# Two chained layers on one core: the second layer's input projection by seven products for half of k

## The chip, the cores and the metric

The kernel runs on 1 core of one Trainium2 chip. The metric is the device time of one execution in microseconds (us): 2892.36 us median of 3 runs (2892.21 to 2892.92). Less is better.

## The reference, cut to what matters

Two layers run one after the other on a sequence of 512 tokens with model width 2048. The first is a gated delta rule layer with cross attention. The second, which the change touches, is this (cut):

```python
u = rmsnorm(h, norm_w[l])                                   # (1, 512, 2048)
proj = jnp.einsum('bsd,dc->bsc', u, w_in[l])                # (1, 512, 8200)
(ml_q, ml_k, ml_v, ml_o, ml_z, ml_i, ml_f,
 hg_q, hg_f, hg_i, hg_g) = jnp.split(proj, split_points, axis=-1)
...
h_a = mlstm_chunkwise(q_a, k_a, v_a, i_pre, f_pre)          # 4 heads
y_a = jax.nn.sigmoid(ml_o) * rmsnorm(h_a) * jax.nn.silu(ml_z)
...
h_b = hgrn2_chunkwise(q_b, k_b, logf_b, i_b)                # 8 heads
y_b = rmsnorm(h_b) * jax.nn.silu(hg_g)
y = jnp.concatenate([y_a, y_b], axis=-1)
h = h + jnp.einsum('bsc,cd->bsd', y, w_out[l])
e = jnp.einsum('bsr,rd->bsd', p[l], w_pe[l])
gate = jax.nn.sigmoid(jnp.einsum('bsd,de->bse', rmsnorm(h), w_pg[l]))
out = rmsnorm(h + gate * e)
```

All in float32.

## The kernel before, in words

Everything is kept transposed: 128 features on the partitions, the 512 tokens (`T`) along the free axis. A projection is a list of jobs. One job (class `Job`) is one output tile of 128 features by 512 tokens, accumulated in one PSUM bank over `kt` tiles of k (16 for the second layer's input projection). To keep float32 accuracy at the speed of the `float32r` type, both operands are split in a high and a low part, hi = float32r(x) and lo = x - hi, and each k takes three matmuls: hi·xh, hi·xl, lo·xh (`_unit`). So a tile of the second input projection is 48 matmuls of 128x512.

Weights come in pieces of `KC` = 4 k-tiles (128x512 elements, 256 KB). `_pump` issues the load of a piece into one of `RAW` = 6 buffers named raw (on the SyncE queue, SP), makes hi by a copy on ScalarE (ACT) and lo by a subtraction on VectorE (DVE), into `SPL` = 5 buffers each.

The order of the work is written out by a planner that runs while the program is built (class `Driver`). It holds a clock for each engine, with a cost for each kind of operation, and issues whichever task of highest priority is ready by these clocks, and otherwise the next matmul unit. So every engine's order of instructions is fixed, and is right to the extent that the costs are. The costs know of no influence of one engine on another. A task is a Python generator; where it says `yield`, the planner may put other work ahead of its next part.

Working tiles (128x512) come from a pool of `NSLOT` = 75 slots, PSUM has 8 banks. The 16 normalised input tiles of the second projection (`X2`), each as hi and lo, hold 32 slots.

The second projection has 65 jobs: the gates i and f (`w_if`, half as wide), 16 tiles for the four mLSTM heads (`ml_task`), 24 for the eight HGRN2 heads (`hg_task`: f, q, i for each head), then 8 `w_mlo`, 8 `w_mlz` and 8 `w_hgg` gate tiles. `scaled` reads a finished bank on DVE and multiplies with the row norm. An `hg_task` goes through seven levels: on each, DVE and ACT make a tile z and TensorE (PE) makes a product named pg from it. Head results stay in slots until the gate tiles have multiplied them (`evac_gate`), and `split_task` makes the operands of the output projection (`Y2`, tiles ph and pl).

GpSimd (POOL) has next to nothing to do in this stage. It sums squares at the start of the kernel (tile xsum).

Of the kernel before, what the change touches and what calls it, by code (L numbers as in the profile page):

```python
# [9 lines left out]
F32 = mybir.dt.float32  # L10
# [13 lines left out]
RAW, SPL = 6, 5  # L24
NSLOT = 75
LV, LP = 0.3, 0.3
AHEAD = 1.5
# [37 lines left out]
class Job:  # L65

    def __init__(self, w, x, evac, n=T, prio=5.0, begin=None, c0=0):
        self.w, self.x, self.evac, self.n, self.prio, self.begin = w, x, evac, n, prio, begin
        self.cols = slice(c0, c0 + n)
        self.kt = w.shape[1]  # L70
        self.narrow = w.shape[2] < 128
        self.ps = None
        self.drop = False

# [8 lines left out]
class Driver:  # L83
# [5 lines left out]
    def __init__(self, tc, wp, psp, sp):  # L89
        self.tc, self.nc, self.wp, self.psp, self.sp = tc, tc.nc, wp, psp, sp  # L90
        self.clk = dict(pe=0.0, act=0.0, dve=0.0, pool=0.0, sp=1.2)
        self.dq = 0.0
        self.tau = 0.0
        self.tasks = []
        self.units = []
        self.pieces = []
        self.i_unit = self.i_dma = self.i_hi = self.i_spl = self.i_mm = 0
        self.spl_end = []
# [6 lines left out]
        self.nslot = 0  # L105
        self.table = None
        self.reader, self._bank = {}, []
        self.small_mm = False
        self.nhead, self.head = 0, None
# [192 lines left out]
    def add(self, *jobs):  # L302

        pcs = {j: [] for j in jobs}
        for c0 in range(0, max(j.kt for j in jobs), KC):
            for j in jobs:
                if c0 >= j.kt:
                    continue
                n = min(KC, j.kt - c0)
                p = len(self.pieces)  # L310
                self.pieces.append((j, c0, n))
                for k in range(c0, c0 + n):
                    self.units.append((j, k, p, k == c0 + n - 1, j is jobs[-1]))

    def _pump(self):
        while self.i_dma < len(self.pieces):
            r = self.i_dma - RAW
            if r >= 0 and (r >= self.i_spl or self.spl_end[r][1] > self.clk["pe"]):
                break
            j, c0, n = self.pieces[self.i_dma]  # L320
            raw = self.wp.tile([128, KC, 128], F32, tag="raw", bufs=RAW, name="raw")
            self.nc.sync.dma_start(out=raw[:, :n, :j.w.shape[2]], in_=j.w[:, c0:c0 + n])
            self.pieces[self.i_dma] = (j, c0, n, raw, self.land(n * 128 * j.w.shape[2]))
            self.i_dma += 1
            if self.i_dma <= self.nhead:
                self.head(self.i_dma)
        while self.i_hi < self.i_dma and self.i_hi < self.i_mm + SPL:
            j, c0, n, raw, tau = self.pieces[self.i_hi]
            if tau > self.clk["pe"] and self.i_hi > self.i_mm:
                break  # L330
            hi = self.wp.tile([128, KC, 128], F32R, tag="hi", bufs=SPL, name="hi")
            self.tau = tau
            m = j.w.shape[2]
            self.act(hi[:, :n, :m], raw[:, :n, :m], AF.Copy)
            self.pieces[self.i_hi] = (j, c0, n, raw, hi, self.tau)
            self.i_hi += 1
        while self.i_spl < self.i_hi:
            j, c0, n, raw, hi, tau = self.pieces[self.i_spl]
            if tau > max(self.clk["pe"], self.clk["dve"]) and self.i_spl > self.i_mm:
                break  # L340
            self.tau = tau
            if j.narrow:
                lo = None
                self.tt(hi[:, :n, 64:], raw[:, :n, :64], hi[:, :n, :64], SUB)
            else:
                lo = self.wp.tile([128, KC, 128], F32R, tag="lo", bufs=SPL, name="lo")
                self.tt(lo[:, :n], raw[:, :n], hi[:, :n], SUB)
            self.pieces[self.i_spl] = (j, c0, n, hi, lo, self.tau)
            self.spl_end.append((self.i_spl, self.tau))
            self.i_spl += 1  # L350

    def _unit_tau(self):

        j, k, p, _, _ = self.units[self.i_unit]
        if p >= self.i_spl or not j.x.f[k].done:
            return None
        t = max(self.pieces[p][5], j.x.f[k].tau)
# [4 lines left out]
        return t  # L362

    def _unit(self):
        j, k, p, last_of_piece, last_job = self.units[self.i_unit]
        self.i_unit += 1
        _, c0, _, hi, lo, _ = self.pieces[p]
# [7 lines left out]
        c = j.cols  # L375
        self.tau = 0.0
        self.mm(j.ps, hi[:, k - c0], xh[:, c], start=(k == 0), stop=False)
        self.tau = 0.0
        self.mm(j.ps, hi[:, k - c0], xl[:, c], start=False, stop=j.narrow and k == j.kt - 1)
        if not j.narrow:  # L380
            self.tau = 0.0
            self.mm(j.ps, lo[:, k - c0], xh[:, c], start=False, stop=(k == j.kt - 1))
        self.tau = self.clk["pe"]
        if last_of_piece:
            self.i_mm += 1
            self.pieces[p] = None
        if j.drop and last_job and (k + 1) % j.x.per == 0:
            self.free(xh, xl)
        if k == j.kt - 1:
            self.tau = self.clk["pe"] + 0.2  # L390
            self.spawn(j.evac(j), j.prio)
# [5 lines left out]
    def run(self):  # L397
        while True:
# [20 lines left out]
            if self.i_unit < len(self.units):  # L419
                ut = self._unit_tau()  # L420
                if ut is not None:
                    if ut <= now:
                        self._unit()
                        continue
                    nxt = ut if nxt is None else min(nxt, ut)
                for i in (self.i_hi, self.i_spl):
                    if i < self.i_dma:
                        u = self.pieces[i][-1]
                        if u > now:
                            nxt = u if nxt is None else min(nxt, u)  # L430
                if self.i_dma < len(self.pieces) and self.i_dma - RAW >= 0 and self.i_dma - RAW < self.i_spl:
                    u = self.spl_end[self.i_dma - RAW][1]
                    if u > now:
                        nxt = u if nxt is None else min(nxt, u)
# [10 lines left out]
def build(ctx: ExitStack, tc: tile.TileContext, A, out):  # L445
# [208 lines left out]
    def x_task():  # L654
# [15 lines left out]
        d.tau = tp  # L670
        f = Fut()
# [22 lines left out]
    def evac_k(e):  # L694
        def gen(job):
# [8 lines left out]
            if i == 1:  # L704
                r = yield from rms([t[:, 0], t[:, 1]], 1.0 / 256, n=NM)
# [533 lines left out]
    def split_task(w, fin, parts, reserve):  # L1239
        for i in range(w, len(fin), WK):  # L1240
# [4 lines left out]
            lo = yield from slot(dt=F32R, name="pl", reserve=reserve - 1)  # L1245
# [82 lines left out]


# [90 lines left out]
    def ml_task(h):  # L1420
# [90 lines left out]
        for a in range(2):  # L1511
            stt(sqs[a], nums[a], nw[:, 2 * h + a:2 * h + a + 1], d2, MUL, MUL)
            give(f_hs[2 * h + a], sqs[a])
        d.free_bank(3)
        free(d2)

    def evac_gate(i, func, last):
        def gen(job):
# [5 lines left out]
            if last:  # L1524
                give(f_hf[i], h)
        return gen

# [64 lines left out]
    def hg_task(h):  # L1592
# [109 lines left out]
        give(f_hs[2 * MLH + h], r)  # L1702
# [45 lines left out]
    def p_task():  # L1748
        yield from need(f_pb)
# [18 lines left out]

    NSP = 3
# [143 lines left out]
    J2 = [Job(A["w_if"][0], X2, evac_if)]  # L1913
    for h in range(MLH):
        for c in (MLH + h, h):
            J2.append(Job(A["w_mlqk"][c], X2, evac_mqk(c)))
        for i in range(2):
            J2.append(Job(A["w_mlv"][2 * h + i], X2, evac_mv(2 * h + i)))
        d.spawn(ml_task(h), 10 + h)
    for h in range(HGH):  # L1920
        J2.append(Job(A["w_hgf"][h], X2, evac_hf(h)))
        J2.append(Job(A["w_hgq"][h], X2, evac_hq(h)))
        J2.append(Job(A["w_hgi"][h], X2, evac_hi(h)))
        d.spawn(hg_task(h), 20 + h)
    for i in range(2 * MLH):
        J2.append(Job(A["w_mlo"][i], X2, evac_gate(i, AF.Sigmoid, False)))
    for i in range(2 * MLH):
        J2.append(Job(A["w_mlz"][i], X2, evac_gate(i, AF.Silu, True)))
    for i in range(HGH):
        J2.append(Job(A["w_hgg"][i], X2, evac_gate(2 * MLH + i, AF.Silu, True)))  # L1930
    d.add(J2[0], J2[1])
    for j in J2[2:-2]:
        d.add(j)
    J2[-1].drop = True
    d.add(J2[-2], J2[-1])
    for w in range(WK):
        d.spawn(split_task(w, f_hf, Y2, 6), 40 + 0.1 * w)
    d.spawn(h1_loader(), 8)
    jo = [Job(A["w_out2"][i], Y2, evac_o2(i), begin=begin_of(f_o2[i])) for i in range(KT)]
    jo0 = jo[0].begin  # L1940

    def begin_o2():
        jo0()
        give(f_pb)

    jo[0].begin = begin_o2
# [7 lines left out]
    d.spawn(p_task(), 39)  # L1954
    je = [Job(A["w_pe"][i], PP, evac_e(i)) for i in range(KT)]
# [4 lines left out]
    for i in range(2, KT - NSP):  # L1960
        d.add(je[i])
# [127 lines left out]
```

## Time and profile before

| what | value |
|---|---|
| median of 3 runs | 2892.36 us |
| the profiled execution's own time | 2891.97 us |
| its span, first to last instruction | 2890.2 us |
| PE busy | 2847.4 us (99%) |
| DVE busy | 1716.1 us (59%) |
| ACT busy | 1389.9 us (48%) |
| POOL busy | 98.0 us (3%) |
| SP's DMA queue, share of 16 engines | 33.7% |

A matmul's duration covers its whole way through the array, and the next one starts before it ends: a 128x512 matmul shows 0.39 us and the next starts 0.227 us later. So the cost of a matmul is the distance between starts, and a busy share of 99% says that something was always under way. "lo<-raw,hi" names an instruction's output tile and its inputs. A releaser is what an engine waited for. Instructions that a helper issues all carry the helper's line.

### The profile page before, as it was taken

Reading aid. Unit: us, or ns where it says so; the run is one execution under the profiler, and the core shown is the slowest. Engines: PE = TensorE matmul, PEld = TensorE weight load, DVE = VectorE, ACT = ScalarE, POOL = GpSimd, SP = SyncE. Lnnn points to the kernel's source line nnn. Section 1 sums busy time; section 2 is a strip of 40 time slices with the busy share of each in tenths; the row PEclk is TensorE's granted clock in tenths of the full one; section 3 lists DMA queues with packets and bytes.
Section 4 is the critical chain, followed back from the end, with each engine's and each line's share of the span. In section 5 each row is a group of like instructions: output and inputs, shape, how many; then the busy total and the mean of one; then the engine's idle time right before and its main releaser. Section 6 shows DMA issues by size and latency. Waiting matters only on the chain. (4 is left out here: it accounts for less than half of the span.)

```text
span 2890.2 us, 41231 instructions
## 1 busy us (share of the span) xinstructions
PE 2847.4 (99%) x15032; PEld 2380.3 (82%) x15032; DVE 1716.1 (59%) x3323; ACT 1389.9 (48%) x2664; POOL 98.0 (3%) x198
## 2 busy tenths in 40 slices
PE   8999999999999999999999999999999999999998
PEld 7877888888888888888888878888888888888887
DVE  6746687778788777645333364556556565444446
ACT  6544545555555555444222344445555565333444
POOL 2000100000000000000000000000000000000001
PEclk9999999999999999999999999999999999999999
DMA  7422323233232322354433433322222222333334
GB/s 238 149 81 95 119 88 99 96 99 101 74 104 95 96 95 95 103 179 124 130 119 119 145 111 108 95 76 84 81 77 81 86 82 91 121 121 111 92 97 150
DMA packets 179020, 311.05 MB, mean 108 GB/s; under 512 B 25344, under 2 KB 32128, under 8 KB 178816
## 3 DMA queue, kind: packets, MB, share of 16 engines
q1 hardware_dynamic: 178816, 308.41, 33.7%
q8 instruction: 118, 1.93, 0.3%
q14 instruction: 86, 0.70, 0.1%
HBM read 292.34 MB, written 15.99 MB: 107 GB/s over the span
## 5 line engine op out<-in xcount | busy, mean ns | idle before, releaser
L155 DVE TENSOR_TENSOR lo<-raw,hi 128x512 fp32r<-128x512 f32 (+1 forms) x956 | 644.1, 686 | 615.7 <-ACT hi L141 602.4
L141 ACT ACTIVATE hi<-raw 128x512 fp32r<-128x512 f32 (+1 forms) x964 | 590.6, 621 | 822.0 <-PE acc L208 688.1
L208 PE MATMUL acc<-xh,hi 128*128 128x512 f32 x1424 | 581.8, 409 | 0.6 <-DVE vb L155 0.6
L208 PE MATMUL acc<-xl,hi 128*128 128x512 f32 x1424 | 555.4, 390 | 0.0
L208 PE MATMUL acc<-xh,lo 128*128 128x512 f32 x1408 | 550.9, 391 | 1.1 <-DVE lo L155 1.1
L208 PE MATMUL acc<-x2h,hi 128*128 128x512 f32 x1040 | 415.4, 399 | 0.0
L208 PE MATMUL acc<-x2l,hi 128*128 128x512 f32 x1040 | 405.3, 390 | 0.0
L208 PE MATMUL acc<-x2h,lo 128*128 128x512 f32 x1024 | 399.7, 390 | 0.0
L208 PEld LDWEIGHTS acc<-xh,lo 128*128 128x128 f32 x1408 | 264.3, 188 | 59.7 <-DVE lo L155 1.9
L208 PEld LDWEIGHTS acc<-xh,hi 128*128 128x128 f32 x1424 | 267.9, 188 | 53.0 <-issue 1.7
L208 PEld LDWEIGHTS acc<-xl,hi 128*128 128x128 f32 x1424 | 268.2, 188 | 51.1 <-issue 1.7
L208 PE MATMUL acc<-ph,hi 128*128 128x512 f32 x768 | 298.8, 389 | 0.0
L208 PE MATMUL acc<-pl,hi 128*128 128x512 f32 x768 | 298.8, 389 | 0.0
L208 PE MATMUL acc<-ph,lo 128*128 128x512 f32 x768 | 298.8, 389 | 0.0
L208 PEld LDWEIGHTS acc<-x2h,hi 128*128 128x128 f32 x1040 | 195.6, 188 | 37.3
L208 PEld LDWEIGHTS acc<-x2l,hi 128*128 128x128 f32 x1040 | 195.8, 188 | 37.0
L208 PEld LDWEIGHTS acc<-x2h,lo 128*128 128x128 f32 x1024 | 192.2, 188 | 41.2
L208 PEld LDWEIGHTS acc<-pl,hi 128*128 128x128 f32 x768 | 144.1, 188 | 30.2
L208 PEld LDWEIGHTS acc<-ph,hi 128*128 128x128 f32 x768 | 144.1, 188 | 29.9
L208 PEld LDWEIGHTS acc<-ph,lo 128*128 128x128 f32 x768 | 144.1, 188 | 29.7
L160 DVE SCALAR_TENSOR_TENSOR cv<-acc,c_dn_conv,cv 128x511 f32<-128x511 f32 x144 | 107.4, 747 | 28.1 <-ACT cv L141 24.4
L155 DVE TENSOR_TENSOR Xb<-Xb,Nb 128x16 f32<-128x16 f32 (+30 forms) x372 | 113.9, 306 | 8.9
(324 smaller groups left out, 3676.6 us busy)
## 6 DMA issues: line engine op xcount, KB each, us to landing
raw<-w_qkv SPq DMA_DIRECT2D x192, 256.0 KB, 3.2
raw<-w_out SPq DMA_DIRECT2D x192, 256.0 KB, 2.9
raw<-w_z SPq DMA_DIRECT2D x128, 256.0 KB, 3.1
raw<-w_pg SPq DMA_DIRECT2D x76, 256.0 KB, 3.2
gR<-dgc SPq DMA_DIRECT2D x48, 256.0 KB, 4.1
raw<-w_k SPq DMA_DIRECT2D x32, 256.0 KB, 5.2
raw<-w_v SPq DMA_DIRECT2D x32, 256.0 KB, 3.5
raw<-w_xq SPq DMA_DIRECT2D x32, 256.0 KB, 3.1
```

The source lines that it names most:

```text
L141: self.nc.scalar.activation(out=out, in_=in_, func=func, **kw)
L155: self._v(eng, 0.07 + n / 960, 0.43 + n / 590).tensor_tensor(out=out, in0=a, in1=b, op=op)
L160: self._v(None, 0.13 + free_size(out) / 960, 0).scalar_tensor_tensor(out=out, in0=a, scalar=s, in1=b, op0=op0, op1=op1)
L208: self.nc.tensor.matmul(out, lhsT=lhsT, rhs=rhs, start=start, stop=stop, is_transpose=True if tr else None)
```

## The change: what it does

**Seven products.** 58 of the 64 full tiles are taken in 29 pairs (`Pair`, `add_pair`). For k-tiles 8 to 15 a pair works as before. For k-tiles 0 to 7 the pair is seen as a product of 2 by 2 blocks: two output tiles by two groups of four k-tiles, times two groups of four k-tiles by two halves of the tokens. In place of eight block products there are seven, of sums and differences of blocks. Each is 4 k-tiles by 3 matmuls of 128x256. Five of them need other accumulators: banks p and q hold two products each, and `_sums` copies both to slots (ACT) and combines them with four DVE operations of 128x256; `scaled` adds the result to the bank before it multiplies.

**Sums of weights.** For each pair four of the eight loaded pieces are combined on POOL by four subtractions (`_top`, 128x512), and the four resulting operands are split on POOL too, by a copy and a subtraction each, into a ring of `TB` = 3 pairs of buffers. Seven pieces are still split on ACT and DVE.

**Sums of inputs.** `x2_sums` makes the combined input blocks once, on POOL, and splits them on ACT and DVE: 16 more slots.

**Room.** The heads' results and the half gated tiles go out to DRAM (`hgs_`) and come back when a gate tile needs them (`gate_loader`) or the output projection does (`h_loader`). The mLSTM gate pairs (o and z of one tile) now stand between the pairs of the HGRN2 heads. `RAW` goes from 6 to 8, `NSLOT` from 75 to 73.

**Order.** Six of the `w_pe` jobs (`NPE`) move ahead of the output projection. `rms`, `x_task` and `evac_k` get a `yield` between their parts.

The core of the diff (left out: the split of `_pump` into records, and what only renames):

```diff
-RAW, SPL = 6, 5
-NSLOT = 75
+RAW, SPL = 8, 5
+NSLOT = 73
+TB = 3
...
+    def add_pair(self, pr):
...
+        u = [(j, c) for c in range(2 * KC, j0.kt, KC) for j in (j0, j1)]
+        usual(*u[0])
+        b11, b12 = load(j0, 0), load(j1, 0)
+        b12.made = False
+        usual(*u[1])
+        b22, b21 = load(j1, KC), load(j0, KC)
+        diff(t1, b12, b11)
+        for q, l in ((0, b11), (5, t1)):
+            product(q, l)
+        diff(t2, b22, t1)
+        diff(b12, b22, b12)
+        for v in u[2:-1]:
+            usual(*v)
+        for q, l in ((3, b22), (6, t2), (7, b12)):
+            product(q, l)
+        diff(t4, b21, t2)
+        usual(*u[-1])
+        for q, l in ((2, b21), (4, t4)):
+            product(q, l)
...
+    def _top(self, op, pe):
...
+            op.hi, op.lo = self.tring[self.i_tp % TB]
+            self.tau = l.tau
+            self.cp(op.hi, l.raw, eng=pool)
+            self.tt(op.lo, l.raw, op.hi, SUB, eng=pool)
...
+        self.tt(dst.raw, x.raw, y.raw, SUB, eng=pool)
...
+    def _punit(self, u):
...
+        for n, (w, x) in enumerate(((pc.hi, xh), (pc.hi, xl), (pc.lo, xh))):
+            self.tau = 0.0
+            self.mm(ps[:, oc], w[:, k], x[:, c], start=first and n == 0,
+                    stop=end and n == 2 and q not in (2, 3))
...
+    def _sums(self, pr):
...
+        self.act(z0, pr.acc["p"], AF.Copy)
+        self.act(z1, pr.acc["q"], AF.Copy)
+        self.free_bank(2)
+        yield
+        for o, x, y in ((z0[:, b], z0[:, a], z0[:, b]), (z1[:, a], z1[:, a], z0[:, b]),
+                        (z0[:, b], z0[:, b], z1[:, b]), (z1[:, b], z1[:, b], z1[:, a])):
+            self.tt(o, x, y, ADD)
...
     def rms(srcs, scale, mul=1.0, n=T):
...
             act(q[:, :n], s, AF.Square)
             sq.append(q)
+        yield
...
+    def x2_sums():
...
+                tt(t, hi, lo, ADD, eng=pool)
...
+            for o, x, y, op in ((s[:, a], u[:, b], v[:, b], ADD), (s[:, b], s[:, a], u[:, a], SUB),
+                                (t[:, a], u[:, a], u[:, b], SUB), (t[:, b], v[:, a], s[:, b], SUB)):
+                tt(o, x, y, op, eng=pool)
...
     def scaled(job):
         r = yield from need(f_r1)
-        t = yield from slot(name="pr")
-        tt(t, job.ps, r, MUL)
+        if job.z is None:
+            t = yield from slot(name="pr")
+            tt(t, job.ps, r, MUL)
+            d.acc_done()
+            return t
+        t = yield from need(job.z)
+        yield
+        tt(t, t, job.ps, ADD)
         d.acc_done()
+        tt(t, t, r, MUL)
         return t
...
+    seq = mls + hgs[:2]
+    hgs = hgs[2:]
+    for i in range(max(len(hgs), len(gts))):
+        seq += hgs[i:i + 1] + gts[i:i + 1]
+    seq += [tuple(gl[i:i + 2]) for i in range(0, HGH - 2, 2)]
+    for i, (j0, j1) in enumerate(seq):
+        d.add_pair(Pair(j0, j1, X2, f_s2, drop=(i == len(seq) - 1)))
```

## Rows read from the trace of the kernel before

**Rows 1.** Part 1 of the page: busy us, share of the span, instructions.
```profile
PE 2847.4 (99%) x15032; PEld 2380.3 (82%) x15032; DVE 1716.1 (59%) x3323; ACT 1389.9 (48%) x2664; POOL 98.0 (3%) x198
```

**Rows 2.** Busy time by stretch: length, then PE, PEld, DVE, ACT, POOL, clock, DMA, GB/s.
```profile
0.00:120.00 120.00, 103.43 (x778) 100.97 (x779) 85.80 (x156) 80.06 (x156) 21.65 (x20) 0.94 0.64 209
120.00:1140.00 1020.00, 1011.17 (x5872) 828.58 (x5871) 739.81 (x1656) 546.00 (x1206) 60.83 (x150) 1.00 0.30 96
1674.00:1735.00 61.00, 58.10 (x260) 47.56 (x258) 41.63 (x72) 26.48 (x50) 0.00 (x0) 1.00 0.33 104
1735.00:2480.00 745.00, 744.22 (x3743) 626.70 (x3742) 420.23 (x716) 382.91 (x647) 4.46 (x12) 1.00 0.27 86
2480.00:2502.00 22.00, 22.00 (x98) 18.22 (x98) 8.14 (x13) 6.96 (x11) 0.00 (x0) 1.00 0.31 99
```

**Rows 3.** The chain that ended last: start us, us, what; its longest piece.
```profile
2440.97 241.44 PE acc L208 x1065
```

**Rows 4.** Timeline of PE: start us, us, instruction; the 256 columns of w_pg.
```profile
2839.83 0.28 PE L208 MATMUL acc<-x3h,hi 128*128 128x256 f32 x1
...
2848.94 0.28 PE L208 MATMUL acc<-x3l,hi 128*128 128x256 f32 x1
```

**Rows 5.** Groups of instructions on POOL, whole run: busy us, mean ns, idle before.
```profile
L155 POOL TENSOR_TENSOR xsum<-xsum,xsq 128x512 f32<-128x512 f32 x15 | 20.8, 1389 | 40.1 <-ACT xsq L141 39.4
L155 POOL TENSOR_TENSOR out<-h1r,gt 128x256 f32<-128x256 f32 x10 | 8.8, 910 | 452.3 <-DVE lo L155 440.5 <-ACT gt L141 11.8
L175 POOL COPY xsum<-xsq 128x512 f32<-128x512 f32 x1 | 0.6, 611 | 12.5 <-ACT xsq L141 12.5
```

**Rows 6.** Groups of instructions on DVE, 1735 to 2480.
```profile
L155 DVE TENSOR_TENSOR lo<-raw,hi 128x512 fp32r<-128x512 f32 x230 | 155.0, 688 | 113.2 <-ACT hi L141 109.8 <-PE acc L208 0.6
L155 DVE TENSOR_TENSOR z<-z,pr 128x256 f32<-128x256 f32 x112 | 42.7, 422 | 32.2 <-ACT z L141 32.2
L155 DVE TENSOR_TENSOR pr<-acc,ssum 128x512 f32<-128x512 f32 x57 | 39.0, 684 | 11.6 <-PE acc L208 11.6
L155 DVE TENSOR_TENSOR z<-b 128x512 f32<-128x512 f32 x56 | 38.0, 678 | 0.0
L155 DVE TENSOR_TENSOR sq<-sq,pr 128x512 f32<-128x512 f32 x21 | 14.5, 692 | 16.7 <-ACT pr L141 16.7
```

**Rows 7.** Timeline of POOL and DVE where both work, near 42.
```profile
41.55 1.29 POOL L155 TENSOR_TENSOR xsum<-xsum,xsq 128x512 f32<-128x512 f32 x1 [11.30 <-ACT xsq L141]
41.97 1.43 DVE L155 TENSOR_TENSOR lo<-raw,hi 128x512 fp32r<-128x512 f32 x1 [0.27 <-ACT hi L141]
42.93 1.62 POOL L155 TENSOR_TENSOR xsum<-xsum,xsq 128x512 f32<-128x512 f32 x1
```

**Rows 8.** Timeline of DVE and PE in one HGRN2 head.
```profile
2104.91 0.76 DVE L155 TENSOR_TENSOR z<-z,pr 128x256 f32<-128x256 f32 x2 [0.55 <-ACT z L141]
2115.42 0.76 DVE L155 TENSOR_TENSOR z<-z,pr 128x256 f32<-128x256 f32 x2 [0.55 <-ACT z L141]
...
2106.40 0.68 PE L208 MATMUL pg<-z 128*64 128x64 f32 x8
2120.97 1.05 PE L208 MATMUL pg<-z 128*128 128x128 f32 x8
```

**Rows 9.** Groups of instructions on ACT, 1735 to 2480.
```profile
L141 ACT ACTIVATE hi<-raw 128x512 fp32r<-128x512 f32 x230 | 141.3, 624 | 169.9 <-PE acc L208 139.5 <-issue 24.3 <-ACT hi L141 1.8
```

**Rows 10.** DMA issues: KB each, median us to landing.
```profile
hscr<-xr SPq DMA_DIRECT2D x16, 256.0 KB, 4.0
h1r<-hscr SPq DMA_DIRECT2D x16, 256.0 KB, 3.6
```

**Rows 11.** Who PE waited for, whole run: us, times, longest.
```profile
PE ss L208 <- ACT qh L141: 7.2, 3, 4.4
PE acc L208 <- ACT mh L141: 6.7, 1, 6.7
PE acc L208 <- DVE lo L155: 3.5, 4, 2.2
```

More of the change, by code (lines that the diff above doesn't have):

```diff
@@ L73, in __init__ @@
         self.drop = False
+        self.z, self.fin, self.stop = None, True, False
+        self.ks = range(self.kt)
+class Pair:
+    def __init__(self, j0, j1, x, comb, drop=False):
+        self.j0, self.j1, self.x, self.comb, self.drop = j0, j1, x, comb, drop
+        for j in (j0, j1):
+            j.z, j.fin = Fut(), False
+        j1.stop = True
+        self.acc = {}
+class PUnit:
+    def __init__(self, pair, q, k, p):
+        self.pair, self.q, self.k, self.p = pair, q, k, p
+class Load:
+    def __init__(self, w, c0, n):
+        self.w, self.c0, self.n = w, c0, n
+        self.raw, self.tau, self.uses, self.end = None, 0.0, 0, None
+        self.made, self.old = w is not None, None
+class Piece:
+    def __init__(self, src, narrow=False, own=True):
+        self.src, self.narrow, self.own, self.ready = src, narrow, own, False
+        self.hi = self.lo = None
+        self.tau = 0.0
+        src.uses += 1
 class Parts:
@@ L105, in __init__ @@
         self.nslot = 0
+        self.pairs = 0
         self.table = None
@@ L302, in add @@
     def add(self, *jobs):
-        pcs = {j: [] for j in jobs}
         for c0 in range(0, max(j.kt for j in jobs), KC):
             for j in jobs:
-                if c0 >= j.kt:
+                if c0 >= j.kt or c0 not in j.ks:
                     continue
                 n = min(KC, j.kt - c0)
-                p = len(self.pieces)
-                self.pieces.append((j, c0, n))
+                self.loads.append(Load(j.w, c0, n))
+                p = Piece(self.loads[-1], j.narrow)
+                self.pieces.append(p)
@@ L312, in add, with load, usual, diff @@
                 for k in range(c0, c0 + n):
                     self.units.append((j, k, p, k == c0 + n - 1, j is jobs[-1]))
+    def add_pair(self, pr):
+        j0, j1 = pr.j0, pr.j1
+        self.pairs += 1
+        for j in (j0, j1):
+            j.ks = range(2 * KC, j.kt)
+        ld = {}
+        def load(j, c):
+            ld[j, c] = Load(j.w, c, KC)
+            self.loads.append(ld[j, c])
+            return ld[j, c]
+        def usual(j, c):
+            p = Piece(load(j, c))
+            self.pieces.append(p)
+            for k in range(c, c + KC):
+                self.units.append((j, k, p, k == c + KC - 1, False))
+        def diff(dst, x, y):
+            self.tops.append((dst, x, y))
+            x.uses += 1
+            y.uses += 1
+            parts[dst] = Piece(dst, own=False)
+        def product(q, l):
+            p = parts.get(l)
+            if p is None:
+                p = Piece(l)
+                self.pieces.append(p)
+            else:
+                self.tops.append(p)
+            for k in range(KC):
+                self.units.append(PUnit(pr, q, k, p))
+        parts = {}
+        t1, t2, t4 = ts = [Load(None, 0, KC) for _ in range(3)]
+        for i, t in enumerate(ts):
+            t.old, self.sums[i] = self.sums[i], t
+        u = [(j, c) for c in range(2 * KC, j0.kt, KC) for j in (j0, j1)]
[17 more added lines that the diff above has]
+            product(q, l)
@@ L326, in _pump @@
                 self.head(self.i_dma)
[L327 to L350, printed above, removed]
@@ L425, in run @@
                     nxt = ut if nxt is None else min(nxt, ut)
[L426 to L432, printed above, removed]
+                for u in self._next_pump():
                     if u > now:
@@ L1244, in split_task @@
             act(hi, y, AF.Copy)
-            lo = yield from slot(dt=F32R, name="pl", reserve=reserve - 1)
+            lo = yield from slot(dt=F32R, name="pl", reserve=lambda: (reserve() if callable(reserve) else reserve) - 1)
             yield
@@ L1512, in ml_task, with evac_gate @@
             stt(sqs[a], nums[a], nw[:, 2 * h + a:2 * h + a + 1], d2, MUL, MUL)
-            give(f_hs[2 * h + a], sqs[a])
         d.free_bank(3)
         free(d2)
-    def evac_gate(i, func, last):
+        yield
+        for a in range(2):
+            d.dma(hgs_[2 * h + a], sqs[a])
+            free(sqs[a])
+            give(f_hm[2 * h + a])
+    gated = [0] * KY
+    def evac_gate(i, func):
         def gen(job):
@@ L1523, in gen, with gate_loader, h_loader @@
             free(t)
-            if last:
+            gated[i] += 1
+            if i >= 2 * MLH:
                 give(f_hf[i], h)
-        return gen
+            elif gated[i] == 2:
+                yield
+                d.dma(hgs_[i], h)
+                free(h)
+                give(f_hg[i])
+        return gen
+    def gate_loader(i):
+        yield from need(f_hm[i])
+        t = yield from slot(name="hl")
+        yield
+        d.dma(t, hgs_[i])
+        give(f_hs[i], t)
+    hgs_ = tc.dram_tile([KY, 128, T], F32, name="hgs")
+    f_hm = [Fut() for _ in range(KY)]
+    f_hg = [Fut() for _ in range(2 * MLH)]
+    f_pd = Fut()
+    def h_loader():
+        yield from need(f_pd)
+        for i in range(2 * MLH):
+            yield from need(f_hg[i])
+            t = yield from slot(name="hm", reserve=8)
+            yield
+            d.dma(t, hgs_[i])
+            give(f_hf[i], t)
     hg = {}
@@ L1927, in build @@
[L1927 to L1935, printed above, removed]
+    d.add(Job(A["w_if"][0], X2, evac_if), mk(MLH))
+    for j in (mk(0), mv(0), mv(1)):
+        d.add(j)
+    mls, hgs, gts = [], [], []
+    for h in range(1, MLH):
+        mls += [(mk(MLH + h), mk(h)), (mv(2 * h), mv(2 * h + 1))]
@@ L1938, in build @@
     d.spawn(h1_loader(), 8)
     jo = [Job(A["w_out2"][i], Y2, evac_o2(i), begin=begin_of(f_o2[i])) for i in range(KT)]
[L1940 to L1946, printed above, removed]
+    je = [Job(A["w_pe"][i], PP, evac_e(i)) for i in range(KT)]
+    for i in range(2, 2 + NPE):
+        d.add(je[i])
+    d.spawn(after(f_pb, p_task(), d), 39)
+    gl[-2].begin = begin_of(f_pb)
+    jo[0].begin = begin_of(f_o2[0])
     d.add(jo[0], jo[1])
```

259 lines of the change are left out of this document (225 added, 34 removed).

## The prediction

> **What bounds the kernel now.** I read the page's first part, then the busy time by stretch, then the chain of waits, and only then single lines. PE is busy 99% of the span, the next engine 59% [rows 1]. A share can hide waits, so the stretches come next: in the second projection (about 1674 to 2502) PE is idle for 2.9 us in the first 61 us and for 0.8 us in the following 745 us, while DVE and ACT work 420 and 383 us of those 745 and POOL 4.5 us [rows 2]. The chain confirms it where nothing else is mixed in: 1065 matmuls of 128x512 in a row take 241.44 us, 0.2267 us each [rows 3]. The stage is bound by the number and width of its matmuls. A matmul taken out of it is worth its distance to the next, as long as everything that feeds PE keeps up.
>
> **The price of half a matmul.** 256 columns do not cost half of 512. From the first to the last row of the stretch of w_pg with 256 columns there are 76 distances in 9.11 us, 0.120 us each [rows 4], each with a new load of weights: against 0.2267 / 2 = 0.1133. The seven products use this narrow form, so part of the eighth is paid back at once.
>
> **What the products save.** For k-tiles 0 to 7 a pair has now 2 tiles x 8 k x 3 = 48 matmuls of 512, 48 x 0.2267 = 10.88 us. After the change it has 7 products x 4 k x 3 = 84 matmuls of 256, 84 x 0.120 = 10.08 us. The gain is 0.80 us a pair, and the other half of k (10.88 us) stays. 29 pairs: -23.2 us. By exact halving it would have been 29 x 12 x 0.1133 = 39 us. The stretch of the pairs (745 us of today) would become 722 us, a pair 20.96 us of its own matmuls.
>
> **What POOL gets.** Per pair 4 subtractions of weights, 4 copies and 4 subtractions for the splits: 8 x 1.389 + 4 x 0.611 = 13.6 us [rows 5], in 20.96 us or more: it fits alone, at 65% at most. The ring of three lets it run ahead: the operand of the second product (after 24 matmuls of 512 and 12 of 256, 6.9 us into the pair) can be made in the pair before. x2_sums is 8 x 1.389 + 16 x 0.910 = 25.7 us once, beside the first five jobs, which are 32 + 4 x 48 matmuls of 512, 50.8 us. Hidden; if not, it is late by at most those 26 us once.
>
> **What DVE and ACT get.** DVE: one split less (-0.69), four operations of 128x256 (4 x 0.42) and two more multiplications in scaled (2 x 0.69): +2.4 us a pair [rows 6], 69 us in all, on 420: some 490 of 722 us, 68%. ACT: two copies more, one less, at 0.62 each [rows 9], so +18 us. In the first layer DVE worked 740 of 1020 us (73%) and PE lost 8.8 us, 0.9% [rows 2]. So by load alone the cost on PE is small; I carry up to 0.9% of 722, 6.5 us, as a bound.
>
> **What they do to each other.** This is the one thing that the trace of the stage can't show, as POOL is idle there. Near 42 us it can be seen: a subtraction of DVE (lo) that starts while POOL adds takes 1.43 us in place of 0.69, and ends 0.56 us after POOL's end; the POOL operation behind it takes 1.62 in place of 1.29 [rows 6, 7]. So the two take turns, a DVE operation is late by up to 0.74 us and a POOL operation by 0.33. The page "SBUF — State Buffer" of the Trainium skill (section "Who interferes with whom") says it as a rule: a Vector instruction with two inputs in SBUF contends with a GpSimd instruction that reads SBUF, one of them blocking for the whole instruction. The trace agrees. What it costs here is bounded from both sides. Below: nothing, if the lateness stays within the lead of what DVE makes. Above: both engines' times add (the slow rival).
>
> The lead I read from the trace. Pieces of weights are made as soon as a buffer is free: of ACT's idle time ahead of hi, 139.5 of 169.9 us ends by PE giving back a buffer [rows 9], so they stand up to four pieces (4 x 12 x 0.2267 = 10.9 us) ahead. For the z of a head the lead is shorter: on the first level DVE ends at 2105.67 and PE takes it at 2106.40, 0.73 us; on the third 2116.18 and 2120.97, 4.8 us [rows 8]. So the first level is the thin place. Its chain has three DVE operations with both inputs in SBUF. If two of them are hit at 0.74 us, it is 1.48 - 0.73 = 0.75 us late, for 8 heads 6 us. PE's order is fixed, so such a wait stands in front of all that follows. I take +6 us; the ends are 0 and the rival below. It lies near the lower end since most leads are several times the lateness.
>
> **The rest.** The trip of the heads' results through DRAM is 14 + 14 transfers, and 8 + 8 for the gated tiles, 44 of 256 KB at about 4 us each [rows 10]; loads are issued when the gate tile begins, some 20 us before it ends. They lie behind weight loads on SP, 8 of which (a whole pair) are ahead. The DMA engines are at 27% of their time in this stretch [rows 2], and 44 x 0.262 MB in 722 us add 16 GB/s to 86. Nothing on the path; if a store holds up SP, the lead of a pair of loads, 21 us, covers it. PSUM: a pair takes four banks, mLSTM heads four (three sums and one passing), so all eight are in use for three heads: a wait of the order of the evacuation, 2 x (0.69 + 0.69) us, at most once a pair in six pairs, 0 to 16 us; I take 0, as p and q are free before the pair ends. The move of six w_pe jobs ahead of the output projection shifts 36 matmuls and adds none: 0, where no wait is seen today around 2502 [rows 2]. The yields in the norms and the deeper prefetch touch the first layer: its waits for ACT's qh, for the first tile and for lo sum to 17.4 us [rows 11], of which 6.7 us is the first load and stays. I take 0, with -5 to +5 as the range: they change an order, and remove no work.
>
> **The sum.** The profiled execution took 2891.97 us, 1.8 us more than its span, and 0.4 us less than the median. 2892 - 23.2 + 6 = 2874.8: I say 2875 us.
>
> **The rivals.**
> *Slower: POOL and DVE exclude each other all the time.* By durations, the DVE operations with both inputs in SBUF in this stretch are lo, the z of both sizes and the gates' products, 155.0 + 42.7 + 38.0 + 14.5 = 250 us [rows 6]; the smaller ones I estimate from the kernel's text at nine of 0.69 us for each of 12 heads, 75 us; the change adds 69: some 394 us. POOL adds 29 x 13.6 = 394. Together 788 us, where PE needs 722. If they can't overlap at all, the stretch is 788 us long, 66 more, and the time is 2892 - 23 + 66 = 2935 us. The point from which it decides is a sum over 722. Against it: in turns, a POOL operation and a DVE operation took 1.62 us together and not 1.29 + 0.69 = 1.98 [rows 6, 7], since start and end of one lie beside the other; at that rate the sum is 788 x 1.62 / 1.98 = 645 us, 89% of the stretch. For it: the heads' stretch is denser than the mean, and at 89% queues are long. By the rule of the Trainium skill cited above, blocking for the whole instruction, this rival would hold in full.
>
> *No difference: the gain is waited away in the pair.* 0.8 us a pair is one late operand. If an operand from POOL, a bank or a slot makes each pair wait once for the length of one hit (0.74 us), 29 x 0.74 = 21 us go and the time is 2890 us. For it: 73 slots, of which 32 + 16 hold inputs and 9 the sums of weights, leave 16, and an HGRN2 head alone takes about ten. Against it: heads have more time than now, 2.5 pairs each (52 us) against three tiles (33 us).
>
> *The change saves nothing on PE*, because 84 loads of weights in place of 48 show. Then a narrow matmul would cost more than 0.130 us. Rows 4 show 0.120 with a load for each, at the same clock: hardly.
>
> **How the numbers follow.** Forecast with its own range, 2864 to 2884: 0.60. Waited away, 2885 to 2900: 0.14. The slow rival, 2900 to 2960: 0.23. Nothing saved on PE: 0.03, within 10 us of 2892. A measurement tells 0.2% (5.8 us) from no change, so faster is below 2886.6 and slower above 2898.1: faster 0.62, same 0.12, slower 0.26. The range: the lower end is the full gain and the 5 us of the first layer, 2864; the upper one takes in the slow rival up to about half its length beyond the even point, 2922, and leaves out some 0.15 above and 0.04 below.
>
> **What would show it.** Right: 128x256 matmuls of acc 0.120 us apart, POOL some 390 us busy between 1735 and 2460, DVE's lo there longer than 0.69 us in the mean with PE idle for no more than 10 us in that stretch, and the stretch about 17 us shorter. Wrong: PE waiting for z, lo or POOL's tiles for 20 us or more, spread over the HGRN2 heads (the slow rival), or a wait of half a us or more in every pair (the second).

## The result, and the profile after

The changed kernel takes 2975.18 us (median of four runs, 2972.39 to 2978.51), the kernel before in the same batch 2892.28 us (2891.68 to 2892.92): a ratio of 1.029, 95% interval 1.0276 to 1.0303. It is 83 us slower. Forecast were 2875 us and at most 2922: sign and range are both wrong.

The first part of the page after answers to [rows 1] (busy us, share of the span, instructions).

```profile
PE 2849.0 (96%) x16076; PEld 2419.7 (81%) x16076; DVE 1997.9 (67%) x3476; ACT 1390.9 (47%) x2694; POOL 581.6 (20%) x570
```

PE is as long busy as before but for 1.6 us, in a span that is 85 us longer. So PE does not have more work; it stands still. Where, the busy time by stretch says, in the columns of [rows 2], cut at the first and the last matmul that reads x2h (the second projection). The kernel before in these cuts:

```profile
1674.70:2501.40 826.70, 823.02 (x4093) 691.39 (x4092) 469.29 (x798) 415.12 (x707) 4.46 (x12) 1.00 0.28 88
2501.40:2890.20 388.80, 375.12 (x1790) 315.96 (x1788) 190.86 (x308) 155.90 (x265) 8.79 (x10) 0.99 0.37 118
```

and the kernel after:

```profile
1665.90:2581.50 915.60, 828.61 (x5125) 735.42 (x5124) 723.17 (x937) 406.92 (x723) 460.81 (x363) 0.98 0.31 92
2581.50:2975.00 393.50, 377.69 (x1802) 317.29 (x1800) 199.69 (x323) 163.30 (x277) 8.79 (x10) 0.99 0.36 116
```

The projection begins 8.8 us earlier (1665.9 against 1674.7), lasts 88.9 us longer, and what is behind it takes 4.7 us more: together the 84.8 us by which the span grew. Within the projection PE was idle for 3.7 us (826.7 - 823.0) and is now idle for 87.0.

Whom PE waits for in the projection is in the table of its waits (us in all, times, longest), which answers to [rows 11]:

```profile
PE pg L249 <- DVE z L196: 22.3, 19, 2.8
PE tr L249 <- DVE pr L196: 11.6, 2, 11.2
PE oh L249 <- DVE u L201: 10.7, 8, 2.8
PE tr L249 <- DVE mcv L210: 10.0, 3, 4.1
PE ss L249 <- DVE ql L196: 8.2, 10, 2.3
```

The table of this stretch has twelve lines, 86.3 us in all. These are the five longest; DVE has 78.2 us, ACT 8.1, and no line names POOL. POOL's own groups (whole run; columns as in [rows 5]) show that its tiles are not late: it stands in front of PE's rings for 289 us.

```profile
L196 POOL TENSOR_TENSOR tp<-wt,tp 128x512 fp32r<-128x512 f32 x87 | 129.4, 1487 | 7.0
L196 POOL TENSOR_TENSOR wt<-raw,wt 128x512 f32<-128x512 f32 x58 | 95.9, 1653 | 0.0
L216 POOL CAST tp<-wt 128x512 fp32r<-128x512 f32 x87 | 72.7, 836 | 289.5 <-PE acc L249 289.4
```

But DVE is slow, and by form. The groups of DVE from 1735 to 2560 answer to [rows 6]:

```profile
L196 DVE TENSOR_TENSOR lo<-raw,hi 128x512 fp32r<-128x512 f32 x202 | 219.4, 1116 | 13.4 <-ACT hi L182 12.2
L196 DVE TENSOR_TENSOR z<-z,z 128x256 f32<-128x256 f32 x168 | 101.3, 630 | 34.1 <-ACT z L182 31.5
L196 DVE TENSOR_TENSOR z<-z,ssum 128x512 f32<-128x512 f32 x56 | 49.2, 879 | 1.9
L196 DVE TENSOR_TENSOR z<-b 128x512 f32<-128x512 f32 x56 | 48.3, 863 | 0.0
L196 DVE TENSOR_TENSOR z<-z,acc 128x512 f32<-128x512 f32 x56 | 37.9, 677 | 0.0
L210 DVE TENSOR_SCALAR z<-z,oml 128x512 f32<-128x512 f32 x8 | 5.9, 738 | 0.0
```

lo takes 1116 ns in the mean, 688 before; the z of 256 columns 630, 422 before; z from b 863, 678 before. The fifth row has the same size and operation, but one of its inputs, acc, lies in PSUM: 677 ns. So it is not all of DVE that is slow, but above all its operations with two inputs in SBUF. Not only these: the z of the sixth row has one input of this size and takes 738 ns, 461 before (named pr there). And a lo is slow only where it meets POOL: of the 202, 78 overlap no operation of POOL and take 684 ns in the mean, the 124 others 1389.

How one hold-up arises, the timeline of POOL and of DVE shows (start us, us, instruction), and then PE's row:

```profile
2218.44 1.55 POOL L196 TENSOR_TENSOR tp<-wt,tp 128x512 fp32r<-128x512 f32 x1
2219.96 1.47 POOL L196 TENSOR_TENSOR wt<-raw,wt 128x512 f32<-128x512 f32 x1
2221.40 1.72 POOL L196 TENSOR_TENSOR raw<-raw 128x512 f32<-128x512 f32 x1
2223.07 1.07 POOL L216 CAST tp<-wt 128x512 fp32r<-128x512 f32 x1
2224.22 1.61 POOL L196 TENSOR_TENSOR tp<-wt,tp 128x512 fp32r<-128x512 f32 x1
...
2220.20 6.18 DVE L196 TENSOR_TENSOR lo<-raw,hi 128x512 fp32r<-128x512 f32 x4
2226.30 0.73 DVE L1978 COPY_PREDICATED at<-lmask,pg 128x512 f32<-128x512 uint8 x1
2226.93 0.67 DVE L196 TENSOR_TENSOR z<-b 128x512 f32<-128x512 f32 x1
2228.14 2.29 DVE L196 TENSOR_TENSOR z<-z,z 128x256 f32<-128x256 f32 x2 [0.54 <-ACT z L182]
...
2230.57 1.13 PE L249 MATMUL pg<-z 128*128 128x128 f32 x8 [2.19 <-DVE z L196]
```

Four lo in a row, 2.75 us of work, take 6.18 us: 1.55 each, about the pace of POOL's operations beside them (1.07 to 1.72). The z of the head stands behind them, its own two operations take 2.29 us in place of 0.76 [rows 8], and PE waits 2.19 us for it. That is one hold-up; all waits for a z are 31.6 of the 86.3 us, and the others were not followed to their start.

### The profile page after: what moved, and what is told of

The parts are those of the page before. It is cut to its first block, busy times and chain, and to the rows that moved or that the text cites. A ratio compares the mean times of both kernels' runs of the same rounds, so it can differ in the third digit from the quotient of the medians.

```text
span 2975.1 us, 44222 instructions
## 1 busy us (share of the span) xinstructions
PE 2849.0 (96%) x16076; PEld 2419.7 (81%) x16076; DVE 1997.9 (67%) x3476; ACT 1390.9 (47%) x2694; POOL 581.6 (20%) x570
## 5 line engine op out<-in xcount | busy, mean ns | idle before, releaser
L196 DVE TENSOR_TENSOR lo<-raw,hi 128x512 fp32r<-128x512 f32 (+1 forms) x927 | 717.7, 790 | 491.9 <-ACT hi L182 469.2
L182 ACT ACTIVATE hi<-raw 128x512 fp32r<-128x512 f32 (+1 forms) x935 | 569.6, 620 | 750.3 <-PE acc L249 626.8
L249 PE MATMUL acc<-x2h,hi 128*128 128x512 f32 (+1 forms) x808 | 301.6, 373 | 0.2 <-ACT hi L182 0.2
L249 PE MATMUL acc<-x2l,hi 128*128 128x512 f32 (+1 forms) x808 | 293.3, 363 | 0.0
L249 PE MATMUL acc<-x2h,lo 128*128 128x512 f32 (+1 forms) x792 | 287.0, 362 | 4.1 <-DVE lo L196 4.1
L249 PEld LDWEIGHTS acc<-x2h,lo 128*128 128x128 f32 x792 | 151.1, 191 | 28.8 <-DVE lo L196 5.0
L249 PEld LDWEIGHTS acc<-x2h,hi 128*128 128x128 f32 x808 | 155.0, 192 | 21.0 <-ACT hi L182 0.4
L249 PEld LDWEIGHTS acc<-x2l,hi 128*128 128x128 f32 x808 | 154.9, 192 | 20.3
L182 ACT ACTIVATE z<-z 128x256 f32<-128x256 f32 (+1 forms) x142 | 60.2, 462 | 197.3 <-DVE z L196 175.4
L249 PE MATMUL acc<-s2h,tp 128*128 128x256 f32 x696 | 141.2, 288 | 2.6 <-DVE z L196 2.6
```

Source lines behind the costliest of these rows:

```text
L182: self.nc.scalar.activation(out=out, in_=in_, func=func, **kw)
L196: self._v(eng, 0.07 + n / 960, 0.43 + n / 590).tensor_tensor(out=out, in0=a, in1=b, op=op)
L249: self.nc.tensor.matmul(out, lhsT=lhsT, rhs=rhs, start=start, stop=stop, is_transpose=True if tr else None)
```

## The experiments

Each ratio is to the kernel before in runs of the same batch. Three theories stood against each other at first. *Contention* (A): POOL's reads of SBUF slow DVE. *Order* (B): POOL's tiles, the banks or the new order make PE wait, whoever is named. *Load* (C): what the change gives DVE to do is too much by itself.

**POOL's weight work left out.** From the second use of each buffer on, POOL skips its copies and subtractions (the products then read old pieces). All matmuls, transfers and work of DVE and ACT stay, in the same order; only what waited for POOL no longer does.

```diff
-            self.cp(op.hi, l.raw, eng=pool)
-            self.tt(op.lo, l.raw, op.hi, SUB, eng=pool)
+            if self.i_tp < TB:
+                self.cp(op.hi, l.raw, eng=pool)
+                self.tt(op.lo, l.raw, op.hi, SUB, eng=pool)
...
```

> The changed kernel, in which POOL's work on the weights of the pairs is left out: only the first use of each buffer is really made, so the products from the second pair on take stale operands, and everything else, PE's, DVE's and ACT's instructions and their order, stays. Theory A (POOL and DVE hinder each other): lo falls back from 1116 ns to about 690 in the stretch of the pairs, PE's waits go, and the time is 2860 to 2875 us, about 105 us under the changed kernel. Rival B (the waits come from the new order, from slots and banks): within 20 us of 2975. Rival C (the heavier DVE load of the change alone): lo stays near 690, but the time stays above 2920.

Measured: 2873.87 us, ratio 0.9937 (0.9922 to 0.9951). The projection in its stretch, and DVE's lo from 1735 to 2465:

```profile
1667.90:2480.20 812.30, 799.94 (x5125) 722.75 (x5124) 536.25 (x937) 410.47 (x723) 19.16 (x24) 0.99 0.35 104
L196 DVE TENSOR_TENSOR lo<-raw,hi 128x512 fp32r<-128x512 f32 x205 | 135.3, 687 | 42.2 <-ACT hi L182 39.5 <-PE ss L249 0.9
```

PE has the same 5125 matmuls and is busy for 799.9 us, 23.1 less than before, and idle for 12.4. lo is back at 687 ns. So 101 of the microseconds of the changed kernel (2975.2 - 2873.9) are there because POOL works. The banks, the new order and DVE's added work are all still in this kernel, and it is faster than the one before: (B), as far as it isn't POOL's tiles, and (C) are out as the cause of the 101 us.

**POOL writes and does not read.** In place of each copy or subtraction one or three fills of the same tile, which read nothing (the products then read constants). The waits of PE and POOL for each other's tiles are back.

```diff
-        self.tt(dst.raw, x.raw, y.raw, SUB, eng=pool)
+        if dst.w is None and dst.old is None:
+            self.tt(dst.raw, x.raw, y.raw, SUB, eng=pool)
+        else:
+            for _ in range(3):
+                pool.memset(dst.raw, 1.0)
...
```

> The changed kernel, in which POOL's copies and subtractions on the weights are replaced from the second pair on by memsets of the same outputs that take about as long in all (one for a copy, three for a subtraction): POOL is as busy and gives its tiles back and forth with PE as before, but reads nothing from SBUF. Products have constant operands. Theory A in the form that only POOL's reads hinder DVE: lo near 690 ns, 2860 to 2880 us. Rival A2 (any POOL instruction hinders DVE, or POOL is simply too late for PE): above 2930 us, in the first case with lo above 1000 ns, in the second with lo near 690 and PE waiting for tp.

Measured: 2879.76 us, ratio 0.9955 (0.994 to 0.997). The busy time from 1735 to 2465, first of this kernel, then of the changed one:

```profile
1735.00:2465.00 730.00, 723.51 (x4787) 660.33 (x4787) 473.02 (x836) 374.09 (x658) 405.50 (x799) 1.00 0.35 102
```

```profile
1735.00:2465.00 730.00, 663.56 (x4224) 593.14 (x4222) 576.28 (x727) 326.42 (x576) 399.02 (x313) 0.98 0.30 89
```

POOL is as busy in both (405 and 399 us). DVE does more operations here (836 against 727) in less time (473 against 576). lo takes 689 ns. So 95.4 of the 101.3 us (2975.2 - 2879.8) go with POOL's reading. Its running, its waits and its writes have the other 5.9; PE waits 5.2 us there once for DVE's mcv, which it doesn't without POOL's work. That POOL keeps raw buffers longer by reading them is no rival: in the changed kernel ACT is idle for 70.7 us ahead of its hi from 1735 to 2560, and all but 1.6 of them end by something else than a load.

**The old kernel with a load on POOL beside it.** 232 splits of the kernel before each start a multiplication on POOL, every second one a copy too. Nobody uses their results; only the buffer of a lo stays taken until POOL has read one column of it.

```diff
+        g.tensor_copy(out=p[:, 0:1], in_=lo[:, 0, 0:1].bitcast(F32))
+        g.tensor_tensor(out=p, in0=p, in1=p, op=MUL)
+        if self.n_side % 2:
+            g.tensor_copy(out=p, in_=p)
...
```

> The kernel before, to which POOL gets the load of the pairs and nothing else: for each of 232 weight pieces of the second projection one multiplication of 128x512 in place on a tile that nobody reads, for every second one also a copy, in all 13.6 us for eight pieces; one slot less. Nobody waits for POOL except the lo buffer, of which it reads one column. Theory A: lo rises from 688 to 900 ns or more in that stretch and the time by 15 to 70 us. Rival B and C: the time stays within 6 us of 2892, since no order and no DVE instruction changes.

Measured: 2936.1 us, ratio 1.0153 (1.0136 to 1.017), as expected; lo takes 798 ns, less than the 900 expected. The stretch, lo in it, and PE's longest wait:

```profile
1735.00:2465.00 730.00, 700.38 (x3476) 586.17 (x3475) 458.03 (x671) 353.33 (x607) 381.11 (x530) 0.98 0.25 80
L156 DVE TENSOR_TENSOR lo<-raw,hi 128x512 fp32r<-128x512 f32 x207 | 159.8, 798 | 40.7 <-ACT hi L142 28.2 <-PE acc L209 4.6 <-POOL side L361 3.2
PE oh L209 <- DVE z L156: 11.9, 3, 4.0
```

With no products, none of the change's order and no operand that POOL makes, 381 us of POOL cost some 44 us (2936.1 / 1.0153 = 2891.9). DVE stands for 3.2 us of these 730 in front of a lo buffer that POOL holds. So contention makes a loss of this kind without the change. Why it is 101 us in the changed kernel is not shown: that has other operations on POOL, more work on DVE, and POOL and PE waiting for each other.

**Half of POOL's work.** The pieces made by POOL are left out for every second pair.

```diff
-            self.cp(op.hi, l.raw, eng=pool)
+            if self.i_tp < TB or self.i_top // 8 % 2 == 0:
+                self.cp(op.hi, l.raw, eng=pool)
...
```

> The changed kernel, in which POOL's work on the weights is left out for every second pair (those products take stale operands); order and all other instructions stay. Full POOL work took 2975 us and none 2874. If the loss grows with every POOL instruction, as turns taken one by one would have it: 2915 to 2935 us. If it is an overload, that comes only when POOL and DVE together have more than the stretch: 2874 to 2895 us.

Measured: 2910.97 us, ratio 1.0063 (1.005 to 1.0077). Half the work costs 37.1 of the 101.3 us: less than in proportion, more than an overload that sets in past a threshold would leave. It lies between both expectations and decides for neither.

**The work on DVE and ACT instead.** Differences and low parts on DVE, high parts on ACT; the planner makes its own order for that.

```diff
-        self.tt(dst.raw, x.raw, y.raw, SUB, eng=pool)
+        self.tt(dst.raw, x.raw, y.raw, SUB)
...
-            self.tt(op.lo, l.raw, op.hi, SUB, eng=pool)
+            self.tt(op.lo, l.raw, op.hi, SUB)
...
```

> The changed kernel, with the four differences and the four low parts of a pair made on DVE and the four high parts on ACT, in the planner's order and with the planner's costs; the output is the full one. Theory A: no POOL beside DVE, 8 subtractions more on DVE for each pair, DVE at about 88% of the stretch of the pairs, lo near 690 ns, 2865 to 2890 us: faster than the kernel before. Rival C (DVE's load is the cause): DVE has 5 us a pair more than in the changed kernel, so the time is 2975 us or more.

Measured: 2923.06 us, ratio 1.0109 (1.0094 to 1.0124), a miss: neither theory's range has it. The stretch, and PE's longest wait in it:

```profile
1735.00:2465.00 730.00, 699.77 (x4561) 635.29 (x4560) 571.86 (x1002) 409.20 (x724) 6.53 (x10) 0.99 0.33 97
PE acc L249 <- ACT hi L182: 10.7, 5, 4.9
```

Its operations have their plain durations (lo 686 ns, the new differences 684), and DVE is 78% busy in place of 65% without POOL (475.8 of 730 us). PE is busy for 28.3 us less of these 730 than there (728.1). So the gain does not survive the same work on DVE and ACT either, with no contention from POOL's pieces. That DVE's load does it is not shown: ACT has more to do as well, and over the projection PE's waits for ACT are 13.6 of 36.0 us.

**Parts of the change alone.** The yields in the kernel before, then the deeper prefetch of raw weights in it (RAW 8, NSLOT 73).

```diff
             sq.append(q)
+        yield
         for q in sq[1:]:
...
```

> The kernel before with one part of the change alone: the yields in rms, x_task and evac_k. In the changed kernel the second projection began 9 us earlier than before (1665.7 against 1674.7). If the yields are the cause: 2880 to 2887 us, and the projection starts about 1667. If the deeper prefetch is the cause: 2890 to 2894.

Measured: 2885.74 us, ratio 0.9976 (0.9966 to 0.9986). The wait of 7.2 us of PE for ACT's qh [rows 11] has gone from its trace; it lay in the first 120 us. The projection begins at 1669.7 us, not quite at the 1667 expected.

> The kernel before with another part of the change alone: eight raw buffers and 73 slots in place of six and 75. If the deeper prefetch is the cause of the first layer's 9 us: 2880 to 2887 us. If the yields are: 2890 to 2894.

Measured: 2893.26 us, ratio 1.0001 (0.9992 to 1.001): nothing.

**Differences made earlier.** DVE makes them in the first layer, and they go through DRAM and come back as plain weights, split as all others; POOL has no part in it. First spread over the first layer:

```diff
+    def presum(prs):
...
+            for o, x, y in ((a, b, a), (b, c, b), (c, c, a), (e, e, c)):
+                yield from d.calm(AHEAD)
+                tt(o, x, y, SUB)
```

> The changed kernel without POOL: the four differences of every pair are made on DVE ahead of time, while the first layer runs, from pieces loaded for it, and stored in DRAM (29 x 8 transfers of 256 KB more), then loaded like any weight piece and split on ACT and DVE; the sums of the inputs are made on DVE too; six raw buffers, 75 slots; full output. DVE gets 29 x 4 x 0.64 = 74 us more in the first layer and as much in the second projection. Theory A: in the projection DVE stays at about 75%, lo near 690 ns, the 23 us of the products come through and the time is 2860 to 2880 us. Rival C (DVE's load): PE waits for DVE in both layers, and the time is above 2892.

Measured: 2934.08 us, ratio 1.0142, out of theory A's range and in that of C. The projection itself became shorter (821 us, with DVE 73% busy), but it begins at 1724 us: the first layer had no room for this work. In one row of that layer PE is idle for 14.0 of 60 us, and the granted clock (third from the end) is 0.77.

```profile
1200.00:1260.00 60.00, 46.02 (x278) 35.15 (x277) 44.81 (x115) 28.95 (x69) 4.53 (x11) 0.77 0.31 97
```

Then begun only at the first layer's output projection (the edit is against the run just shown; a load of a difference not yet made is now waited for):

```diff
-    d.spawn(after(f_ab, presum(prs), d), 50)
+    d.spawn(after(f_ob[0], presum(prs), d), 9.5)
...
```

> As e8, but the differences of the weights are made from the first tile of the first layer's output projection on, where DVE is at 43%, and not in the first layer, in which e8 lost 57 us (its second projection began at 1724 and not at 1667); a load that is not yet made is waited for by the planner. If the products' gain is there once POOL is silent and DVE has room: the projection begins at 1667 to 1672, takes 805 to 822 us, and the time is 2868 to 2886 us. If DVE's load is a bound of its own even without POOL: over 2892 us.

Measured: 2886.47 us, ratio 0.9982 (0.9973 to 0.9991): between the two expected ranges; faster than the kernel before by 0.2%, yet no more than the yields alone, which it contains; of the kernels of this study that compute everything, these two are the fastest.

```profile
1668.80:2495.50 826.70, 808.75 (x5136) 727.05 (x5135) 628.37 (x1108) 476.45 (x847) 4.64 (x12) 0.99 0.49 153
```

The projection takes as long as before: PE's matmuls are 14.3 us less busy, and it is idle 14.3 us more; its longest waits are for DVE's lo (11.2 us in eight). DVE is at 76%; ACT and the DMA engines have more to do as well (49% of the DMA engines' time against 28%).

**A planner that knows.** The planner that writes the order gets an estimate of the mean lateness of DVE and POOL as cost; as the memory asks for it, RAW is 5 and NSLOT 76, and the changed kernel with these sizes alone is its partner.

```diff
+        if self.maxacc == 4 and self.pairs:
+            x = 0.25 if eng is not None else 0.0 if in_psum(a) or in_psum(b) else 0.07 + n / 1420
...
```

> The changed kernel with its planner told of the mean lateness while pairs run: 0.43 us more for a DVE operation of 128x512 with both inputs in SBUF, 0.25 for a POOL operation of two inputs, 0.20 for a POOL copy; five raw buffers and 76 slots, as the planner finds no way with fewer slots. If the loss comes from an order that rests on too low costs: 50 us or more under e11 (the same buffers without the costs). If it comes from the work that POOL and DVE can only do in turns, no order helps: within 25 us of e11, and lo above 1000 ns.

> The changed kernel with five raw buffers and 76 slots and nothing else, for comparison with e10: 2965 to 2990 us if the number of raw buffers does not matter.

Measured: 2994.43 us (ratio 1.0357) with the costs, 3012.19 (1.0417) without. An order planned for the lateness gives back 17.8 us, and lo takes 913 ns in it (1009 in the partner; more than 1000 was expected). This new order leaves most of the loss; that no order avoids it is not shown. The partner is a miss: three raw buffers fewer (and three slots more) cost the changed kernel 37 us, where two more had given the old one nothing.

## Why the prediction was wrong, point by point

*The price of half a matmul* was right. PE's timeline in a stretch of the changed kernel without a wait has 11 distances in 1.30 us, 0.118 us each, against 0.120 in [rows 4].

```profile
2428.93 0.27 PE L249 MATMUL acc<-x2h,hi 128*128 128x256 f32 x1
...
2430.23 0.28 PE L249 MATMUL acc<-x2h,lo 128*128 128x256 f32 x1
```

*What the products save* was right: 23.2 us were predicted, and with POOL still the projection has 23.1 us less of PE. Of this, 14.4 us arrive (826.7 to 812.3). Most of the rest goes in one place, beside the first jobs, where I had taken nothing: one wait of 9.8 us for DVE's pr, when the first pieces start on POOL (they are made there too); before it was 2.4 us, and with the pieces on DVE and ACT, but the sums of x still on POOL, it is 2.7. The row of the kernel without POOL's work (us in all, times, longest):

```profile
PE tr L249 <- DVE pr L196: 10.2, 2, 9.8
```

*What POOL gets* was right in that the ring keeps its tiles on time; its size was 394 us for 29 pairs and is 459 (the groups of its weight work summed), since a subtraction takes 1487 to 1653 ns and a copy 814 to 836, not 1389 and 611 [rows 5]. *What DVE gets* was right as a count: 68% predicted, 65% measured with POOL's work left out.

***What they do to each other* is the step that failed.** I took +6 us; the runs show 101. The mechanism and its sizes were those of the prediction: two engines that take turns, at 1.5 to 1.6 us a turn (1.62 was read near 42 us). The same section of the Trainium skill ("SBUF — State Buffer", "Who interferes with whom") holds that a VectorE instruction with two inputs in SBUF contends with a GpSimd instruction that reads SBUF and not with one that only writes it; the traces agree, with lo at 689 ns beside fills and 1116 beside reads, and with 405 us of fills at 2879.8 us and 399 us of copies and subtractions at 2975.2. What failed is the argument from leads. I read leads of 0.73 to 10.9 us in a trace in which DVE was 56% busy, and set one or two hits of 0.74 us against them. But a hit is no single event: from 1735 to 2560 POOL has 78 runs of operations without a pause over 0.15 us, three operations long in 42 of them, six or more in 27, and a lo that meets one costs 1.39 us in the mean in place of 0.69. In the hold-up shown the lead was used up by four lo ahead of a z, and PE, whose order is fixed, stood in front of the z.

*The slow rival* named the right engines at a wrong price and chance (2935 us, 0.23), and the sign that it gave came: PE waiting for z for more than 20 us. What I held against it, 645 us of turns in 722 and so 89%, compares a sum with the length of the stretch, and that does not decide: even its 788 us without any overlap give 2935 us, 40 short of the measured time. The time is lost where PE stands in its fixed order, not where an engine is full. Without POOL's pieces the projection kept 14.4 us of the products' gain with DVE 66% busy in it, 5.4 at 73%, nothing at 76% (differences made earlier, twice), and lost 18 us at 77% (pieces on DVE and ACT). That is the order of DVE's load, but these kernels differ in more than that. *No difference: waited away in the pair* named a wait per pair for POOL's operand, a bank or a slot; no wait names POOL, and without POOL's work, with the same banks and slots, PE is idle for 12.4 us in the whole projection: that rival is out. *Saves nothing on PE* is out too.

*The rest*: the first layer was taken at 0, within 5; it was -8.8 in the changed kernel, and the yields alone bring -6.5 (2892.3 to 2885.7): a term mis-sized but of the right kind. The prefetch in the old kernel is nothing, as taken. What is behind the projection costs 4.7 us more, with 2.6 us of PE: 12 more matmuls lie behind the last one that reads x2h.

Still open: how the 101 us divide. PE's idle time is 74.6 us more than without POOL (87.0 against 12.4); the other 28.7 us of the stretch are a longer busy time of the same matmuls. A part of that is the granted clock: by the trace's record of it PE is busy for 35.7 us of the projection at 0.50, and without POOL's work for 5.9. A matmul of 512 columns stands 0.42 us from the next there in place of 0.23 (shown below), so by estimate some 14 of the 28.7 us are the clock's. By another estimate some 9 are the ends of matmuls in front of waits: there are 61 waits against 6, and ahead of each a matmul shows its whole 0.39 us and not 0.23. The rest is open. Not taken apart either is why five raw buffers cost the changed kernel so much.

## What to carry to other kernels

An engine that stands idle in a trace is not free: before work is moved to GpSimd, list what VectorE does there with two inputs in SBUF, and price each such operation that meets a reading GpSimd operation by a trace in which both work (here 1.39 us in place of 0.68). A lead is read against the whole run of operations ahead of the late one and not against one hit, as all that stands behind it in TensorE's fixed order waits too. A gain of less than 1% is easily waited away: it was gone in both runs of this case with VectorE 76 to 78% busy, though that its load alone did it is not shown. Leaving one engine's work out, with the order of all else kept, splits such a result into its gain and its price in one run.

## What the hardware did that was not expected

A wait can cost more than its length. After the 2.77 us in which PE waited for DVE's u, the granted clock fell, and it rose again only after PE had worked at the lower level. The busy time in stretches of 2 us (clock in the third column from the end):

```profile
2419.00:2421.00 2.00, 1.34 (x8) 1.00 (x7) 2.00 (x2) 0.00 (x0) 2.00 (x2) 1.00 0.15 46
2421.00:2423.00 2.00, 0.00 (x0) 0.00 (x0) 2.00 (x4) 0.00 (x0) 1.25 (x1) 1.00 0.48 146
2423.00:2425.00 2.00, 1.89 (x8) 1.60 (x9) 1.90 (x6) 0.89 (x2) 0.00 (x0) 0.89 0.51 162
2425.00:2427.00 2.00, 2.00 (x8) 1.67 (x7) 1.97 (x5) 1.03 (x1) 0.00 (x0) 0.50 0.53 170
2427.00:2429.00 2.00, 2.00 (x9) 1.65 (x9) 1.30 (x3) 1.40 (x2) 0.00 (x0) 0.76 0.00 0
```

At 0.50 (1.2 GHz) the matmuls of 512 columns stand 0.42 us apart, in place of 0.23. Eleven times in the projection the clock fell so, for 44.4 us in all; in the projection of the kernel before, with waits of 2.4 us at most, it never did. Not every wait of this length does it: behind this one the clock stayed at 1.00, and the matmuls of 512 columns follow at 0.23 us.

```profile
2203.75 0.65 PE L249 MATMUL pg<-z 128*64 128x64 f32 x8 [2.77 <-DVE z L196]
...
2207.18 0.39 PE L249 MATMUL acc<-x2h,lo 128*128 128x512 f32 x1
2207.41 0.40 PE L249 MATMUL acc<-x2h,hi 128*128 128x512 f32 x1
```

What makes the difference no run here shows.
